# Casting and splitting two weights by one instruction, from pages kept in two hand-run regions

## The chip, the cores and the metric

The kernel runs on one core of a Trainium2 chip. The metric is the device time of one execution in microseconds (us). TensorE is PE in the profile, its weight loads PEld; VectorE is DVE, ScalarE is ACT, GpSimd is POOL, and SyncE is SP. SP and POOL issue the DMAs.

## The reference

One layer of an encoder on 256 tokens of width 2048, all in float32: a SwiGLU feed-forward block (FFN, inner width 5632), a mixer with two branches (chunked mLSTM and stick-breaking attention) merged by gates, a second FFN, and an input embedding behind a gate. A layer norm stands behind the first three.

```
x = layer_norm(ALPHA * x + 0.5 * swiglu(x, ffn1_w1, ffn1_w3, ffn1_w2))
proj = x @ w_in                        # all branches and both gates
y_m, y_sb = mlstm(...), stick_breaking(...)
merged = sigmoid(ga) * (y_m @ w_up_m) + sigmoid(gb) * (y_sb @ w_up_sb)
x = layer_norm(ALPHA * x + merged @ w_out)
x = layer_norm(ALPHA * x + 0.5 * swiglu(x, ffn2_w1, ffn2_w3, ffn2_w2))
x = x + sigmoid(x @ w_ple_gate) * (p @ w_ple_proj)
```

Weights are 528 MB of reads, each used once for 256 tokens.

## The kernel before, in words

**The arithmetic.** A float32 product is made of three matmuls of type fp32r: the activation and the weight are each split into a high part (a cast to fp32r) and a low part (the rest), and high x high, high x low, low x high are added in PSUM (L1331, L1332, L1333). A weight here is a raw page of 128 x 1024 elements (two blocks of 128 rows by 512 columns). ScalarE casts it into the high page (L1275), VectorE subtracts that from the raw page into the low page (L1279). TensorE then runs 6 matmuls on it for each of the two token halves; a product of two matrices that share the activations runs in a seven-product scheme (`seven`), in which each weight is used for one unit of 6 matmuls, and in which sums of raw pages are weights too. Such a sum is made by VectorE (L371) or by a load that adds onto a raw page that is in SBUF (`plus_load`, issued by POOL, L377). The load that adds can only be issued when the split of the page's former content is done.

**The order of the work.** The program is a list of units, written out by hand (`program`), in which side work is woven into main work (`weave`); small steps are put in by a table of delays (`DELAY`, `Sched`). Before a unit its weight is split. After each unit `splits_due` splits further weights, as long as fewer than a limit stand ready: `HELD` gives for each stage how many raw pages and how many split weights may be held at a time, for example 11 and 6 in the FFNs. Within 6 weights of a stage's end, 4 raws and 11 splits are the limit. For the first 8 weights no more than 3 are split ahead. Each engine takes its instructions in the order in which they are written.

**The pages.** All of this lies in 51 pages of 4 KB a partition, in one pool: raw pages, high and low pages, and also `big` tiles (residuals, gates, norms), `actT` tiles (activations, transposed and split). The pool hands a page out when it is free. In the mixer, ymT (the output of the mLSTM branch, four `actT` tiles) is put away in DRAM and loaded again shortly before it is used (`put_ym_away`, `bring_ym_back`, L889). That load is written just ahead of the units that read it. PSUM has 8 banks, for sums of matmuls (`mm`) and for transposes (`ms`).

Of the kernel before, what the change touches and what calls it, by code (L numbers as in the profile page):

```python
# [8 lines left out]
F32 = mybir.dt.float32  # L9
# [4 lines left out]
P = 128  # L14
# [8 lines left out]
EPS = 1e-5  # L23
COL = 512

PAGES = 51
TEMP_BUFS = 6


HELD = {"ffn": (11, 6), "mix": (6, 6), "woven": (9, 6), "wide": (11, 6)}  # L30
RAW_EDGE, SPLIT_EDGE = 4, 11
EDGE = 6

# [92 lines left out]
        return self.left.get((c, tt)) == 0  # L126


class Raw:


    def __init__(self, src, cols):
        self.src, self.cols, self.tile, self.early = src, cols, None, False


class Weight:
# [52 lines left out]
def kernel(  # L189
# [14 lines left out]
    temp_pool = ctx.enter_context(tc.tile_pool(name="temp", bufs=TEMP_BUFS))  # L204
    small = ctx.enter_context(tc.tile_pool(name="small", bufs=4))
    ps_pool = ctx.enter_context(tc.tile_pool(name="ps", bufs=PSUM_BUFS, space=bass.MemoryType.PSUM))
    ctx.enter_context(tc.manual_schedule())

    sched = Sched()
# [16 lines left out]
    def big(shape=(P, 1024)):  # L226
        return page_pool.tile(list(shape), F32, name="big", tag="page")
# [487 lines left out]
    def sb_columns(ps, t, heads):  # L715
# [3 lines left out]
        nc.scalar.copy(stage[:, :n], ps[:, :n])  # L719
        sched.spaced(sb_turn(t, stage, heads), DELAY["sbt"], BANK_GAP)  # L720

    def sv_dest(k, t):
        if ("sv", t) not in st:
            st["sv", t] = big()
        return st["sv", t][:, k * COL:(k + 1) * COL]

    def sv_ready(k, t):
# [253 lines left out]
    def stick(h):  # L981
        yield from wait(*[(n, t, h) for n in ("sq", "sk", "sv") for t in range(TT)])
        due = max(sched.now, st.get("stick", 0.0))
        st["stick"] = due + STICK_GAP
        yield bank(due - sched.now)
        q, k = st["sq", "T", h // 4][:, h % 4], st["sk", "T", h // 4][:, h % 4]
        ps = misc([P, 3 * P])
        for s in range(2):
            nc.tensor.matmul(ps[:, 256 * s:256 + P * s], k[:, s * P:(s + 1) * P], q[:, s * P:], start=True, stop=True)  # L989
        z, sp = temp(), temp()  # L990
        n = slice(0, 3 * P)
        activate(z[:, n], ps[:], ACT.Copy, scale=DS ** -0.5)
# [24 lines left out]
        ps = misc([P, S])  # L1017
        for s in range(2):
            nc.tensor.matmul(ps[:, P * s:], st["sv", s][:, h * DS:(h + 1) * DS], z[:, 256 * s:256 + P * s],  # L1019
                             start=(s == 0), stop=(s == 1))  # L1020
        parts = [(ysbT.get(h // 4, t)[:, :, h % 4], ps[:, t * P:(t + 1) * P]) for t in range(TT)]
        for dst, src in parts:
            nc.scalar.copy(dst[:, 0], src)
        for dst, src in parts:
            nc.vector.tensor_tensor(out=dst[:, 1], in0=src, in1=dst[:, 0], op=ALU.subtract)  # L1025
        for t in range(TT):
            ysbT.mark(h // 4, t, 1)
        drop()

    def in_sequence(gens):  # L1030
        for g in gens:
# [53 lines left out]

    def merge_turn(g, t):
        transposed(merged(g, t), mergedT, g, t)
        return
        yield

# [12 lines left out]
    def gate_dest(g):  # L1103
        def dest(k, t):
            if (g, t) not in gt:
                gt[g, t] = big()
            return gt[g, t][:, k * COL:(k + 1) * COL]
        return dest

# [6 lines left out]
    program.append(lambda: sched.spawn(in_sequence([gated(h) for h in range(HM)])))  # L1116
    gate = branch(0, 1)
    main = v(0) + v(1) + sb(8, 9, 2, 3) + sb(10, 11, 4, 5) + [Mode("wide")] + sb(12, 13, 6, 7) + sb(14, 15) + [lambda: sched.spawn(lane())] + branch(0, 0) + gate[:4] + bring_ym_back(gate[4:] + ups(0)) + ups(1) + ups(2)
    mode("woven")
    program.extend(weave(main, in_line([both7(w_in, sq0 + 2 * HS * DS, sq0 + 2 * HS * DS + COL, x1T, sv_dest, sv_ready, later),  # L1120
                                   both7(w_in, 3072, 3072 + COL, x1T, mo_dest, mo_ready, every), pair(1), pair(2), pair(3)])))
# [104 lines left out]
    pos = {"load": 0, "split": 0, "at": 0, "raw": 0}  # L1226

    def at_edge(j):
        return any(-EDGE <= j - e < EDGE for e in edges)
# [10 lines left out]
    def loads(most=len(raws)):  # L1240
        while pos["load"] < most and pos["raw"] < (4 if pos["at"] < 6 else limits(pos["split"])[0]):
            j = pos["load"]
            r = raws[j]
            r.tile = page_pool.tile([P, 2, COL], F32, name="raw", tag="page")
            for ks in pieces(j):
                at = 0
                for src in r.src:
                    n = src.shape[-1]
                    nc.sync.dma_start(out=r.tile[:, ks, at:at + n], in_=src[:, ks])
                    at += n  # L1250
                if j == 0 and ks.start == 0:
                    load_x(0, 1)
            pos["load"] += 1
            pos["raw"] += 1

    def make(j):
# [5 lines left out]
        if w.make and not w.made and not w.by_load and all(r.tile is not None for r in w.loads):  # L1262
            w.make()
            w.made = True

    def split_one():
# [5 lines left out]
        splits[j] = [page_pool.tile([P, 2, COL], F32R, name="split", tag="page") for _ in range(2)]  # L1272
        hi, lo = (h[:, :, :w.cols] for h in splits[j])
        for ks in pieces(j):
            nc.scalar.copy(hi[:, ks], r[:, ks])  # L1275
            make(j + 1)
            if weights[min(j + 1, len(weights) - 1)].made or not weights[min(j + 1, len(weights) - 1)].make:
                make(j + 2)
            nc.vector.tensor_tensor(out=lo[:, ks], in0=r[:, ks], in1=hi[:, ks], op=ALU.subtract)  # L1279
        pos["split"] += 1  # L1280
        for f in w.soon:
            assert f.raw.tile is not None
            f.make()
            f.made = True
        pos["raw"] -= len(w.frees)
        for r in w.frees:
            r.tile = None
# [25 lines left out]
    for u in program:  # L1313
        if isinstance(u, (Boundary, Mode)):
            continue
        if not isinstance(u, Unit):
            u()
            continue
        sched.until(lambda: u.act.ready(u.chunk, u.tt))
        j = u.tile.index  # L1320
        pos["at"] = max(pos["at"], j)
        while pos["split"] <= j:
            split_one()
        if u.start:
            u.acc["ps"] = ps_pool.tile([P, COL], F32, name="mm", tag="ps")
        ps = u.acc["ps"][:, :u.cols]
        a, w = u.act.tiles[u.chunk, u.tt], splits[j]
        for k in range(2):
            hi, lo = a[:, 0, u.sub + k], a[:, 1, u.sub + k]
            first, last = u.start and k == 0, u.stop and k == 1  # L1330
            nc.tensor.matmul(ps, hi, w[0][:, k, :u.cols], start=first, stop=False, skip_group_check=u.onto)  # L1331
            nc.tensor.matmul(ps, hi, w[1][:, k, :u.cols], start=False, stop=False, skip_group_check=u.onto)  # L1332
            nc.tensor.matmul(ps, lo, w[0][:, k, :u.cols], start=False, stop=last, skip_group_check=u.onto)  # L1333
        sched.now += 6 * 0.2161 * u.cols / COL
        u.tile.uses -= 1
        if u.tile.uses == 0:
            splits.pop(j)
        if u.stop:
            u.done(ps, u.tt)
        sched.run()  # L1340
        splits_due()
# [27 lines left out]
```

## Time and profile before

| | |
|---|---|
| median of 3 runs | 2165.42 us (2163.1 to 2165.61) |
| the profiled execution, own time | 2164.03 us |
| its span, first to last instruction | 2162.3 us, so 1.7 us lie around it |
| DVE busy | 1897.6 us (88%) |
| ACT busy | 1344.6 us (62%) |
| loads by POOL that add onto a page | 140 in the FFNs, 38 in the mixer |
| HBM | 527.85 MB read, 247 GB/s over the span |

Busy time is the sum of an engine's instructions; a group's row names the line of the kernel, the engine, the operation, what is written from what, how often, the busy time, the mean duration in ns, and the idle time of the engine just before these instructions with what ended most of it. Rows of the timeline begin with the start and the duration in us. TensorE's ends are modelled, and its matmuls overlap, so the distance from one start to the next is its pace. Loads of `w_in` are issued from 641 to 1222 us and those of `w_out` from 1240 to 1327 us, which is the mixer; the FFNs lie before and behind it, and loads of `w_ple_gate` begin at 2024 us.

### The profile page before, as it was taken

To read this page: it belongs to the slowest core of one execution; us is meant where nothing else is said; L and a number is where in the kernel's file an instruction comes from. 1 tells how busy PE (TensorE), PEld (TensorE's weight loads), DVE (VectorE), ACT (ScalarE), POOL (GpSimd) and SP (SyncE) were. 2 spreads that over 40 slices of the span, in tenths; PEclk is the share of its full clock that TensorE was granted. 3 is DMA by queue.
4 is the path that set the end of the run, shared out by engine and by line. 5 is a ranking of instruction groups with operands and counts; after the bars stand their busy time and mean duration, and the time that the engine had idled before them with its cause. 6 is when DMAs were issued, how large, how long until landed. Compare 5 with 4: busy or idle time off the path is not lost.

```text
span 2162.3 us, 27685 instructions
## 1 busy us (share of the span) xinstructions
PE 2153.1 (100%) x9798; PEld 1782.0 (82%) x9798; DVE 1897.6 (88%) x2096; ACT 1344.6 (62%) x1663; POOL 218.2 (10%) x186
## 2 busy tenths in 40 slices
PE   9999999999999999999999999999999999999999
PEld 7888888888888888888888888888888888888887
DVE  6899999999998898887888975799999999999974
ACT  7656656666665765677866563556656656666572
POOL 0111111111000000101011000011111111110000
PEclk9999999999999999999999999999999999999999
DMA  9899899999994667978898976579989999999642
GB/s 350 220 272 271 248 269 277 273 277 269 266 316 148 211 217 217 244 212 208 263 276 264 274 259 206 200 191 277 267 245 279 277 272 270 265 273 301 233 168 86
DMA packets 283179, 535.98 MB, mean 248 GB/s; under 512 B 17144, under 2 KB 34464, under 8 KB 283040
## 3 DMA queue, kind: packets, MB, share of 16 engines
q1 hardware_dynamic: 234624, 440.87, 60.0%
q0 software_dynamic: 48416, 93.33, 24.0%
q8 instruction: 77, 1.26, 0.2%
q14 instruction: 62, 0.51, 0.1%
HBM read 527.85 MB, written 6.29 MB: 247 GB/s over the span
## 4 chain that ended last, share of the span: by engine, by line
PE 91%; DVE 4%; issue 3%; DMA 2%; ACT 0%; POOL 0%; SPq 0%; DVEq 0%; POOLq 0%; ACTq 0%
PE mm L1331 29%; PE mm L1333 29%; PE mm L1332 29%; DMA raw<-in_ffn_w_dram 2%; DVE split L1279 2%; PE ms L298 1%; PE ms L524 0%; DVE actT L293 0%; POOL raw L377 0%; DVE raw L371 0%; PE ms L911 0%; PE ms L1019 0%; PE ms L989 0%; PE ms L926 0%; ACT split L1275 0%
## 5 line engine op out<-in xcount | busy, mean ns | idle before, releaser
L1275 ACT CAST split<-raw 128x1024 fp32r<-128x1024 f32 (+1 forms) x1089 | 1089.5, 1043 | 516.9 <-DMA raw<-in_ffn_w_dram 185.8
L1279 DVE TENSOR_TENSOR split<-raw,split 128x1024 fp32r<-128x1024 f32 (+1 forms) x1089 | 1277.1, 1210 | 136.6 <-ACT split L1275 128.5
L1331 PE MATMUL mm<-split,actT 128*128 128x512 f32 x3064 | 1201.2, 392 | 0.9 <-DVE actT L1025 0.9
L1333 PE MATMUL mm<-split,actT 128*128 128x512 f32 x3064 | 1187.7, 388 | 0.6 <-DVE actT L305 0.6
L1332 PE MATMUL mm<-split,actT 128*128 128x512 f32 x3064 | 1186.1, 387 | 0.4 <-DVE split L1279 0.4
L1333 PEld LDWEIGHTS mm<-split,actT 128*128 128x128 f32 x3064 | 575.1, 188 | 121.5 <-DVE actT L305 1.8
L1331 PEld LDWEIGHTS mm<-split,actT 128*128 128x128 f32 x3064 | 575.7, 188 | 115.5 <-ACT big L243 1.1
L1332 PEld LDWEIGHTS mm<-split,actT 128*128 128x128 f32 x3064 | 575.8, 188 | 114.5 <-DVE split L1279 1.7
L377 POOL DMA_DIRECT2D raw<-in_ffn_w_dram x140 | 169.7, 1440 | 1202.8 <-DVE split L1279 780.0
L371 DVE TENSOR_TENSOR raw<-raw 128x1024 f32<-128x1024 f32 x190 | 231.4, 1219 | 1.6
L377 POOL DMA_DIRECT2D raw<-in_w_in_dram x38 | 46.0, 1428 | 502.6 <-DVE split L1279 432.8
L300 ACT CAST actT<-ms 128x512 fp32r<-128x512 f32 x60 | 35.1, 586 | 73.6 <-PE ms L298 69.2
L649 DVE SCALAR_TENSOR_TENSOR big<-mm,big 128x512 f32<-128x512 f32 x112 | 76.3, 683 | 3.3 <-PE mm L1333 3.3
L597 DVE TENSOR_TENSOR temp<-mm,temp 128x512 f32<-128x512 f32 x108 | 73.1, 686 | 1.7 <-PE mm L1333 0.3
L305 DVE TENSOR_TENSOR actT<-ms,actT 128x512 fp32r<-128x512 f32 x60 | 40.9, 685 | 14.4 <-ACT big L304 9.3
L243 ACT ACTIVATE temp<-mm 128x512 f32<-128x512 f32 (+1 forms) x36 | 20.3, 569 | 49.9 <-PE mm L1333 49.9
L293 DVE TENSOR_TENSOR actT<-temp,actT 128x512 fp32r<-128x512 f32 x40 | 26.5, 687 | 17.3 <-ACT actT L292 17.2
L239 ACT ACT_TABLE_LOAD x30 | 38.5, 1283 | 0.5
L1191 DVE TENSOR_TENSOR temp<-temp,big 128x512 f32<-128x512 f32 (+1 forms) x10 | 5.8, 582 | 26.4 <-ACT temp L243 26.4
L292 ACT CAST actT<-temp 128x512 fp32r<-128x512 f32 x40 | 23.9, 620 | 8.0 <-DVE temp L316 7.4
L243 ACT ACTIVATE rstd<-mv,eps 128x1 f32<-128x1 f32 x6 | 1.8, 294 | 41.8 <-DVE mv L507 41.8
L1134 DVE SCALAR_TENSOR_TENSOR big<-big,mm 128x512 f32<-128x512 f32 x8 | 5.5, 686 | 25.3 <-PE mm L1333 25.3
(138 smaller groups left out, 613.1 us busy)
## 6 DMA issues: line engine op xcount, KB each, us to landing
raw<-in_ffn_w_dram SPq DMA_DIRECT2D x527, 512.0 KB, 7.0
raw<-in_w_in_dram SPq DMA_DIRECT2D x144, 512.0 KB, 5.1
raw<-in_ffn_w_dram POOLq DMA_DIRECT2D x140, 512.0 KB, 9.9
raw<-in_w_in_dram POOLq DMA_DIRECT2D x38, 512.0 KB, 8.4
raw<-in_w_out_dram SPq DMA_DIRECT2D x32, 512.0 KB, 5.3
raw<-in_w_ple_gate_dram SPq DMA_DIRECT2D x32, 512.0 KB, 5.0
raw<-in_w_in_dram SPq DMA_DIRECT2D x56, 256.0 KB, 4.1
raw<-in_w_up_m_dram SPq DMA_DIRECT2D x16, 512.0 KB, 6.3
```

The lines of the kernel that those rows point to most:

```text
L239: nc.scalar.preload_act_table_set(table[0])
L300: nc.scalar.copy(dst[:, 0], ps[:])
L305: nc.vector.tensor_tensor(out=dst[:, 1], in0=ps[:], in1=dst[:, 0], op=ALU.subtract)
L371: nc.vector.tensor_tensor(out=out.tile[:, :, :cols], in0=a.tile[:, :, :cols], in1=b.tile[:, :, :cols], op=ALU.add)
L377: nc.gpsimd.dma_start(out=out.tile[:, :, :cols], in_=src, accum_op=ALU.add)
L597: nc.vector.tensor_tensor(out=out, in0=a, in1=b, op=op)
L649: nc.vector.scalar_tensor_tensor(out=xs, in0=ps, scalar=0.5, in1=xs, op0=ALU.mult, op1=ALU.add)
L1275: nc.scalar.copy(hi[:, ks], r[:, ks])
L1279: nc.vector.tensor_tensor(out=lo[:, ks], in0=r[:, ks], in1=hi[:, ks], op=ALU.subtract)
L1331: nc.tensor.matmul(ps, hi, w[0][:, k, :u.cols], start=first, stop=False, skip_group_check=u.onto)
L1332: nc.tensor.matmul(ps, hi, w[1][:, k, :u.cols], start=False, stop=False, skip_group_check=u.onto)
L1333: nc.tensor.matmul(ps, lo, w[0][:, k, :u.cols], start=False, stop=last, skip_group_check=u.onto)
```

## The change

Of the 51 pages, 10 raw pages and 12 split pages are taken out of the pool and become two tiles of their own, `raws` and `splits`, which a free list (`Region`) hands out by number; the pool keeps 29. Two weights that follow each other, both of full width and both in pages of `raws`, are cast by one ScalarE instruction over both pages (L1371) and subtracted by one VectorE instruction (L1373); an access pattern with the distance of the two pages as its step makes that possible. Such a pair is split when two weights' room is free. A weight that doesn't qualify is split alone (L1349, L1351), as before. Two page-sized tiles of the mixer (the attention's `sv` and one gate tile) lie in `raws` for a while. The number of raws in one stretch of the mixer ("wide") goes from 11 to 9.

```diff
+RAWS = 10
+SPLITS = 12
+PAGES = 51 - RAWS - SPLITS
-HELD = {"ffn": (11, 6), "mix": (6, 6), "woven": (9, 6), "wide": (11, 6)}
+HELD = {"ffn": (11, 6), "mix": (6, 6), "woven": (9, 6), "wide": (9, 6)}
+class Region:
+    def take(self, n, like=None):
+        at = [self.free.pop(0) for _ in range(n)]
+        if like:
+            at.sort(reverse=like[0] > like[1])
+        return at
+    def give(self, pages):
+        self.free += [p for p in pages if p is not None]
+    def both(self, at):
+        a, b = sorted(at)
+        return self.tile[:, a:b + 1:b - a]
...
+    def lent(name):
+        st["page", name], = raw_pages.take(1)
+        pos["keep"] = int(name != (2, 0))
+        return raw_pages.tile[:, st["page", name]]
...
-            r.tile = page_pool.tile([P, 2, COL], F32, name="raw", tag="page")
+            if len(raw_pages.free) > pos["keep"]:
+                r.page, = raw_pages.take(1)
+                r.tile = raw_pages.sheet(r.page)
+            else:
+                r.tile = page_pool.tile([P, 2, COL], F32, name="raw", tag="page")
...
+    def two(j):
+        if j == 0 or j + 1 >= len(weights) or at_edge(j) or at_edge(j + 1):
+            return False
+        a, b = weights[j:j + 2]
+        if min(a.cols, b.cols) < COL or None in (a.raw.page, b.raw.page) or a.raw is b.raw:
+            return False
+        ahead(j)
+        return whole(j) and whole(j + 1)
+
+    def split_two():
+        j = pos["split"]
+        at = [w.raw.page for w in weights[j:j + 2]]
+        his, los = split_pages.take(2, at), split_pages.take(2, at)
+        r, hi, lo = raw_pages.both(at), split_pages.both(his), split_pages.both(los)
+        nc.scalar.copy(hi, r)
+        ahead(j + 2)
+        nc.vector.tensor_tensor(out=lo, in0=r, in1=hi, op=ALU.subtract)
...
+        for k in range(2):
+            through(j + k)
+        loads()
 
     def splits_due():
         most = pos["at"] + 3 if pos["at"] < 8 else len(weights)
-        while pos["split"] < most and len(splits) < limits(pos["split"])[1]:
-            split_one()
+        while pos["split"] < most:
+            room = limits(pos["split"])[1] - len(splits)
+            if pos["split"] + 1 < most and two(pos["split"]):
+                if room < 2 or len(split_pages.free) < 4:
+                    break
+                split_two()
+            elif room < 1:
+                break
+            else:
+                split_one()
```

Of the 1071 splits of full pages, 906 go into 453 pairs and 165 stay alone (counted in the built program, on ScalarE and on VectorE alike). TensorE's instructions are the same, in the same order. Three places show what moves on the engines around it; numbers tell tiles apart, and in brackets stand the engines and queues that an instruction waits for.

VectorE at the start of the kernel, before: `L305` are the low parts of the activations, `L1279` the low parts of weights 0 (in two halves), 1, 2, 3.

```order
L305 TENSOR_TENSOR actT_120<-ms_115,actT_120 128x512 [waits PE_49,Activation_49]
L1279 TENSOR_TENSOR split_126<-raw_99,split_125 128x512 [waits DMAHW1_49,Activation_49]
L1279 TENSOR_TENSOR split_126<-raw_99,split_125 128x512 [waits DMAHW3_49,Activation_49]
L305 TENSOR_TENSOR actT_138<-ms_133,actT_138 128x512 [waits PE_49,Activation_49]
L1279 TENSOR_TENSOR split_143<-raw_103,split_142 128x1024 [waits DMAHW4_49,Activation_49]
L1279 TENSOR_TENSOR split_149<-raw_107,split_148 128x1024 [waits DMAHW7_49,Activation_49]
L305 TENSOR_TENSOR actT_177<-ms_172,actT_177 128x512 [waits PE_49,Activation_49]
```

The same place now:

```order
L332 TENSOR_TENSOR actT_118<-ms_113,actT_118 128x512 [waits PE_49,Activation_49]
L1351 TENSOR_TENSOR splits_73<-raws_72,splits_73 128x512 [waits DMAHW1_49,Activation_49]
L1351 TENSOR_TENSOR splits_73<-raws_72,splits_73 128x512 [waits DMAHW3_49,Activation_49]
L332 TENSOR_TENSOR actT_133<-ms_128,actT_133 128x512 [waits PE_49,Activation_49]
L1373 TENSOR_TENSOR splits_73<-raws_72,splits_73 128x2048 [waits DMAHW7_49,DMAHW4_49,Activation_49]
L332 TENSOR_TENSOR actT_164<-ms_159,actT_164 128x512 [waits PE_49,Activation_49]
```

Weights 1 and 2 are one instruction, and it waits for both loads, that on queue DMAHW4 and that on DMAHW7.

SP in the mixer, at the last of the four loads that bring ymT back, before:

```order
L1249 DMA raw_10027<-in_w_up_sb_dram 128x2x512 [waits DMAHW0_49,DVE_49,PE_49]
L1249 DMA raw_10039<-in_w_in_dram 128x2x512 [waits DMAHW1_49,DMASW3_49,DVE_49]
L1249 DMA raw_10072<-in_w_up_sb_dram 128x2x512 [waits DMAHW2_49,PE_49]
L889 DMA actT_10074<-ymaway_91 128x1024 [waits DMAHW3_49,PE_49]
L1249 DMA raw_10093<-in_w_in_dram 128x2x512 [waits DMAHW4_49,PE_49]
```

The same place now, on SP:

```order
L1296 DMA raw_8017<-in_w_in_dram 128x2x512 [waits PE_49]
L1296 DMA raws_72<-in_w_up_sb_dram 128x2x512 [waits DMAHW0_49,DMASW3_49]
L924 DMA actT_8045<-ymaway_93 128x1024 [waits DMAHW7_49,DVE_49]
L1296 DMA raws_72<-in_w_in_dram 128x2x512 [waits DMAHW2_49]
L1296 DMA raws_72<-in_w_up_sb_dram 128x2x512 [waits DMAHW3_49]
```

and on VectorE, the instructions up to the one for which this load waits:

```order
L398 TENSOR_TENSOR raws_72<-raws_72,raw_8017 128x1024 [waits DMAHW7_49]
L1373 TENSOR_TENSOR splits_73<-raws_72,splits_73 128x2x1024 [waits DMAHW6_49,Activation_49]
L452 TENSOR_TENSOR big_7957<-mm_7771,big_7957 128x512 [waits DVE_49]
L458 TENSOR_SCALAR big_7957<-big_7957,mm_7746 128x512 [waits DVE_49]
L452 TENSOR_TENSOR raws_72<-mm_7820,raws_72 128x512 [waits PE_49]
L1373 TENSOR_TENSOR splits_73<-raws_72,splits_73 128x2048 [waits DMAHW0_49,Activation_49]
L1351 TENSOR_TENSOR splits_73<-raw_8017,splits_73 128x1024 [waits Activation_49]
```

The load waited for a matmul before; now it waits for VectorE's split of `raw_8017`, whose pool page it gets.

TensorE in the mixer, where a PSUM bank is handed on, before:

```order
L1332 MATMUL mm_7879<-split_8085,actT_6990 128x512
L1333 MATMUL mm_7879<-split_8084,actT_6990 128x512
L733 MATMUL ms_8179<-ident_76,temp_8129 128x128 [waits Activation_49]
L733 MATMUL ms_8179<-ident_76,temp_8129 128x128 x3
L1331 MATMUL mm_8193<-split_8065,actT_6044 128x512 [waits DVE_49]
```

and now:

```order
L1432 MATMUL mm_6242<-splits_73,actT_5536 128x512
L1433 MATMUL mm_6242<-splits_73,actT_5536 128x512
L768 MATMUL ms_6491<-ident_78,temp_6444 128x128 [waits Activation_49]
L768 MATMUL ms_6491<-ident_78,temp_6444 128x128 x3
L1431 MATMUL mm_6499<-splits_73,actT_4735 128x512 [waits PE_49,Activation_49]
```

The sum `mm_6499` now gets the bank of the transposes `ms_6491` that stand right ahead of it, and waits for ScalarE to copy them out; before it got another bank, freed by VectorE.

More of the change, by code (lines that the diff above doesn't have):

```diff
@@ L1028, in stick @@
         drop()
+        st["sticks"] = st.get("sticks", 0) + 1
+        if st["sticks"] == HS:
+            back(("sv", 0))
     def in_sequence(gens):
@@ L1225 @@
     splits = {}
-    pos = {"load": 0, "split": 0, "at": 0, "raw": 0}
+    pos = {"keep": 0, "load": 0, "split": 0, "at": 0, "raw": 0}
     def at_edge(j):
@@ L1264, in make, with through, whole, ahead @@
             w.made = True
+    held = {}
+    def through(j):
+        w = weights[j]
+        for f in w.soon:
+            assert f.raw.tile is not None
+            f.make()
+            f.made = True
+        pos["raw"] -= len(w.frees)
+        for r in w.frees:
+            raw_pages.give([r.page])
+            r.tile = r.page = None
+    def whole(j):
+        w = weights[min(j, len(weights) - 1)]
+        return w.made or not w.make
+    def ahead(j):
+        make(j)
+        if whole(j):
+            make(j + 1)
     def split_one():
@@ L1271, in split_one @@
         r = w.raw.tile[:, :, :w.cols]
-        splits[j] = [page_pool.tile([P, 2, COL], F32R, name="split", tag="page") for _ in range(2)]
+        if len(split_pages.free) > 1:
+            held[j] = split_pages.take(2)
+            splits[j] = [split_pages.sheet(n) for n in held[j]]
+        else:
+            splits[j] = [page_pool.tile([P, 2, COL], F32R, name="split", tag="page") for _ in range(2)]
         hi, lo = (h[:, :, :w.cols] for h in splits[j])
@@ L1275, in split_one @@
             nc.scalar.copy(hi[:, ks], r[:, ks])
-            make(j + 1)
-            if weights[min(j + 1, len(weights) - 1)].made or not weights[min(j + 1, len(weights) - 1)].make:
-                make(j + 2)
+            ahead(j + 1)
             nc.vector.tensor_tensor(out=lo[:, ks], in0=r[:, ks], in1=hi[:, ks], op=ALU.subtract)
         pos["split"] += 1
[L1281 to L1287, printed above, removed]
+        through(j)
+        loads()
[16 more added lines that the diff above has]
+        for k in range(2):
+            held[j + k] = [his[k], los[k]]
+            splits[j + k] = [split_pages.sheet(n) for n in held[j + k]]
+        pos["split"] += 2
+        for k in range(2):
+            through(j + k)
         loads()
```

22 lines of the change are left out of this document (18 added, 4 removed).

## The prediction

> **What bounds the kernel now.** I read the page first: busy time by engine and the chain that ended last.
>
> ```profile
> span 2162.3 us, 27685 instructions
> PE 2153.1 (100%) x9798; PEld 1782.0 (82%) x9798; DVE 1897.6 (88%) x2096; ACT 1344.6 (62%) x1663; POOL 218.2 (10%) x186
> ...
> PE 91%; DVE 4%; issue 3%; DMA 2%; ACT 0%; POOL 0%; SPq 0%; DVEq 0%; POOLq 0%; ACTq 0%
> ```
>
> TensorE is in work for 2153.1 of 2162.3 us, and 91% of the chain is its. A modelled end could hide gaps, so I read its waits next (line, who was waited for, us in total, times, longest).
>
> ```profile
> PE ms L1209 <- DVE ones L247: 1.1, 1, 1.1
> PE mm L1331 <- DVE actT L1025: 0.9, 1, 0.9
> PE ms L298 <- DMA big<-in_x_dram: 0.7, 1, 0.7
> PE mm L1333 <- DVE actT L305: 0.6, 2, 0.3
> PE mm L1332 <- DVE split L1279: 0.4, 1, 0.4
> PE ms L298 <- DVE actT L305: 0.4, 1, 0.4
> ```
>
> These are all, 4.1 us together, 1.8 of them before the first product; only 0.4 us is a wait for a split. Last, TensorE's pace, from its timeline in the mixer and in a stretch where VectorE has little to do.
>
> ```profile
> 1150.58 0.39 PE L1331 MATMUL mm<-split,actT 128*128 128x512 f32 x1
> 1151.26 0.39 PE L1331 MATMUL mm<-split,actT 128*128 128x512 f32 x1
> ...
> 1320.24 0.39 PE L1331 MATMUL mm<-split,actT 128*128 128x512 f32 x1
> 1320.92 0.39 PE L1331 MATMUL mm<-split,actT 128*128 128x512 f32 x1
> ...
> 1296.00:1350.00 54.00, 54.00 (x239) 44.45 (x238) 29.75 (x32) 22.78 (x23) 0.00 (x0) 1.00 0.63 205
> ```
>
> From L1331 to the next L1331 are three matmuls in 0.68 us both times, 0.227 us each, although in the second stretch VectorE is busy for only 29.75 of 54 us, ScalarE for 22.78. TensorE runs at its own pace, which the splitting doesn't touch; time saved on ScalarE and VectorE can only win from the 4.1 us. A measurement of this kernel tells about 0.2%, 4.3 us. What can move the time is whether a split still comes in time.
>
> **The pairs.** Their durations come from two instructions that stand back to back.
>
> ```profile
> 245.13 2.36 DVE L1279 TENSOR_TENSOR split<-raw,split 128x1024 fp32r<-128x1024 f32 x2
> ...
> 1152.59 2.01 ACT L1275 CAST split<-raw 128x1024 fp32r<-128x1024 f32 x2 [3.32 <-PE mm L1332]
> ...
> L1275 ACT CAST split<-raw 128x1024 fp32r<-128x1024 f32 (+1 forms) x1089 | 1089.5, 1043 | 516.9 <-DMA raw<-in_ffn_w_dram 185.8 <-DVE raw L371 155.3 <-PE mm L1332 76.5
> L1279 DVE TENSOR_TENSOR split<-raw,split 128x1024 fp32r<-128x1024 f32 (+1 forms) x1089 | 1277.1, 1210 | 136.6 <-ACT split L1275 128.5 <-PE mm L1332 2.9 <-DMA raw<-in_w_in_dram 2.3
> ```
>
> A pair costs at most 2.36 us on VectorE and 2.01 us on ScalarE; I take 2.28 and 1.95. The saving, 0.06 to 0.14 us by 453 pairs, some 30 to 60 us on each engine, is work beside TensorE's and counts nothing. [...] What a pair does cost is lateness: its first weight is ready only when both raws have landed and both are cast and subtracted, 0.9 + 1.07 us later than alone.
>
> **The start: +4.8 us.** Weights 1 and 2 become a pair.
>
> ```profile
> 8.57 1.05 ACT L1275 CAST split<-raw 128x1024 fp32r<-128x1024 f32 x1
> 11.74 1.05 ACT L1275 CAST split<-raw 128x1024 fp32r<-128x1024 f32 x1 [2.12 <-DMA raw<-in_ffn_w_dram]
> ...
> 9.66 1.22 DVE L1279 TENSOR_TENSOR split<-raw,split 128x1024 fp32r<-128x1024 f32 x1 [0.35 <-ACT split L1275]
> ...
> 10.90 0.48 PE L1331 MATMUL mm<-split,actT 128*128 128x512 f32 x1
> 11.22 0.39 PE L1332 MATMUL mm<-split,actT 128*128 128x512 f32 x1
> ```
>
> Weight 1 was cast at 8.57 and used at 10.90 (high part) and 11.22 us (low part). The raw of weight 2 lands at 11.74: ScalarE waited for it. The loads stand in the same order, so the pair is cast from 11.74 to 13.7 and subtracted to 16.0 us: L1332 starts 16.05 - 11.22 = 4.8 us later. No gap stands behind it that could take this back, since the later waits for L305 (0.6 us) hang on transposes that TensorE itself makes. Bounds 3.8 (that 0.6 and small restarts absorbed) and 5.
>
> **The last ymT load: +10 us.** It now waits for VectorE's split of `raw_8017`, whose cast waits for the last matmul on `mm_8128`, the one ahead of the first reader of the loaded tile. So TensorE stops while a cast, a split and a load run one after the other.
>
> ```profile
> 1141.48 0.42 SPq L889 DMA_DIRECT2D actT<-ymaway  x1
> ...
> DMA to landing us min/median/max: 4.7/5.8/6.9
> ...
> raw<-in_w_in_dram SPq DMA_DIRECT2D x144, 512.0 KB, 5.1
> ...
> 1150.63 0.68 DVE L425 TENSOR_TENSOR big<-mm,big 128x512 f32<-128x512 f32 x1
> ...
> L371 DVE TENSOR_TENSOR raw<-raw 128x1024 f32<-128x1024 f32 x190 | 231.4, 1219 | 1.6
> ```
>
> Before, it was issued at 1141.48 and its tile first read at 1151.26 (the L1331 quoted above): 9.8 us for 5.8, no wait. Now, from the end of the matmul: cast 1.05, split 1.21, load 5.8 and an estimated 0.2 for four hand-overs (cast to split took 257.76 - 256.67 - 1.05 = 0.04 in the rows further down), 8.3 us, with the fastest load 7.1. VectorE comes later than that: `raw_8017` is issued 42 matmuls, 9.5 us, ahead and lands 5.1 later, 4.4 us before the stop; then VectorE still has a sum (L371's kind, 1.22), a pair (2.28), three of L425's kind (3 x 0.65) and a pair (2.28), 7.7 us, so that it reaches the split 3.3 us behind the stop, 2.2 behind the cast. With that 8.3 becomes 10.5; some of it will overlap, I take 10, bounds 7 and 12. The stop gives what is queued behind on SP more time than it loses. [...]
>
> **The PSUM hand-over: +1 us.** `mm_6499` waits for two copies of the kind L738, of 0.37 us each, and for two hand-overs.
>
> ```profile
> L738 ACT COPY big<-ms x16: 344/372/380, 737.6 to 1061.4; 128x256 f32<-128x256 f32 x16
> ```
>
> That is 0.74 + 0.3, 1 us, more if a pair is on ScalarE (bound 2). A second hand-over of this kind stands where TensorE already waited 0.9 us for L1025: nothing.
>
> **The loads that add: +9 us.** In the FFNs a chain runs split, load that adds, cast, split, matmul.
>
> ```profile
> 246.71 2.44 POOL L377 DMA_DIRECT2D raw<-in_ffn_w_dram  x2 [32.01 <-DVE split L1279]
> ...
> 256.67 1.05 ACT L1275 CAST split<-raw 128x1024 fp32r<-128x1024 f32 x1 [2.88 <-DMA raw<-in_ffn_w_dram]
> ...
> 257.76 1.23 DVE L1279 TENSOR_TENSOR split<-raw,split 128x1024 fp32r<-128x1024 f32 x1 [2.32 <-ACT split L1275]
> ...
> 262.28 0.39 PE L1332 MATMUL mm<-split,actT 128*128 128x512 f32 x1
> ```
>
> From the issue at 246.71 to the cast are 10.0 us, the low part is ready at 258.99, TensorE reads it at 262.28: 3.3 us to spare, in one of the tightest. With pairs the chain grows by 1.07 + 0.9 + 1.07 = 3.0 us, and counted in matmuls of the unchanged order, from the one that frees a page to the one that needs the load, it has 17 us where it had 18.3 (the shortest in each). 3.3 - 3.0 - 1.3 = -1.0 us: the tightest are late by about 1 us. There are 9 blocks of seven products in each FFN; a stop in one lets its other chains catch up, so I count half of 18 at 1 us each: 9. Bounds 0 (the shorter queue on VectorE gives it back) and 18 blocks x 2 = 36.
>
> **The sum.** 4.8 + 10 + 1 + 9 = 25 us onto the profiled execution's own 2164.0 (span and 1.7 around it): 2189, and as the median of the runs lies 1.4 us above that execution, 2190.
>
> **Rivals.** *A, the loads that add decide* (chance 0.18): if landing goes late with the fuller bursts of two raws, all 18 blocks lose 1.5 to 2.5 us: 27 to 45 in place of 9, 2208 to 2226. For it, in the page's slices, the busy share of the DMA engines in tenths:
>
> ```profile
> DMA  9899899999994667978898976579989999999642
> ```
>
> In most of the FFNs' slices it is 0.9 or more. Against: the same bytes in the same time.
> *B, only the mixer and start count* (0.16): the chains hold as before, and the ymT load comes at its lower bound: 3.8 + 7 + 1, 2177.
> *C, not slower: TensorE's pace* (0.06): 0.227 us a matmul might hold waits for SBUF, behind ScalarE and VectorE. With 42% fewer split instructions it would have to fall by 2.7 ns to 0.2243 to win 25 us over the 9192 products and end at 2165; beyond that, faster. Against it: the pace was the same at 29.75 us of VectorE in 54. [...]
> The rest (0.60) is the forecast, 2190, its own range 2180 to 2207.
>
> **The numbers.** Range 2174 to 2212: it takes in B, the forecast and the lower part of A. Slower by over 0.2% holds for the forecast, A and B, 0.94, less something for a step read wrongly: 0.90; within 0.2%: 0.05; faster: 0.05.
>
> **What would show it.** In the changed profile: L1332 of weight 1 near 16 us; a wait of TensorE for the DMA from `ymaway` of 7 to 12 us, the longest of all; a wait of about 1 us for L773; waits for L1371 and L1373 in the FFNs of some 9 us in all; VectorE's busy time down by 30 to 70 us; matmuls still 0.227 us apart. I am wrong if TensorE's waits stay near 4 us, or if a single one above 3 us stands elsewhere.

## The result, and the profile after

The changed kernel takes 2321.8 us (median, 2320.4 to 2322.8), the one before in the same session 2165.5: ratio 1.072, 95% interval 1.070 to 1.074. It is slower by 156 us; the forecast was 2190 with a range of 2174 to 2212. Times in this text are medians of executions that agree within 0.5%; a single one that took 7770 us, of a later version (a pair's subtract as two instructions), is left out.

The page of the changed kernel, its span, its busy time by engine, and the chain that ended last:

```profile
span 2318.7 us, 26169 instructions
PE 2238.2 (97%) x9798; PEld 1785.9 (77%) x9798; DVE 1873.0 (81%) x1643; ACT 1300.2 (56%) x1210; POOL 217.2 (9%) x186
...
PE 54%; issue 17%; DVE 13%; DMA 11%; ACT 4%; POOL 1%; SPq 0%; ACTq 0%; POOLq 0%; DVEq 0%
```

VectorE and ScalarE have 25 and 44 us less to do, as the change meant. TensorE does the same 9798 matmuls and is busy for 85 us longer, and its share of the chain that ended last is 54% where it was 91%. Its waits (line, who was waited for, us in total, times, longest):

```profile
PE mm L1432 <- DVE splits L1373: 56.0, 52, 2.2
PE mm L1431 <- DMA actT<-ymaway: 8.1, 1, 8.1
PE mm L1431 <- ACT splits L1371: 3.1, 3, 2.2
...
PE mm L1431 <- ACT big L773: 0.7, 1, 0.7
```

L1371 and L1373 are the cast and the subtract of a pair, L773 the copy of transposes out of PSUM. TensorE waited for a split 0.4 us before, and now 56 us in 52 places. But all its waits come to some 75 us of 156, so I looked at the distance between matmuls that wait for nothing, in the timeline of the mixer:

```profile
1160.03 0.39 PE L1431 MATMUL mm<-splits,actT 128*128 128x512 f32 x1
...
1166.33 0.39 PE L1431 MATMUL mm<-splits,actT 128*128 128x512 f32 x1
```

Nine rounds of three matmuls lie between the two rows: 6.30 us / 27 = 0.2333 us each, and 0.227 before. This holds throughout: of all distances of 0.220 to 0.245 us between the starts of 512-column products, the mean is 227.2 ns over 8,695 before and 233.2 over 8,495 after. That is some 6.0 ns x 8,500 = 51 us.

One place in an FFN shows the stops (start, duration, engine; in brackets the idle time ahead and what ended it):

```profile
641.12 1.91 ACT L1371 CAST splits<-raws 128x2048 fp32r<-128x2048 f32 x1 [7.33 <-DMA raws<-in_ffn_w_dram]
643.06 2.29 DVE L1373 TENSOR_TENSOR splits<-raws,splits 128x2048 fp32r<-128x2048 f32 x1 [4.91 <-ACT splits L1371]
645.40 0.50 PE L1432 MATMUL mm<-splits,actT 128*128 128x512 f32 x1 [1.82 <-DVE splits L1373]
...
656.55 1.23 DVE L398 TENSOR_TENSOR raws<-raws,raw 128x1024 f32<-128x1024 f32 x1
657.94 1.91 ACT L1371 CAST splits<-raws 128x2048 fp32r<-128x2048 f32 x1 [5.22 <-DVE raws L398]
659.89 2.29 DVE L1373 TENSOR_TENSOR splits<-raws,splits 128x2048 fp32r<-128x2048 f32 x1 [0.91 <-ACT splits L1371]
662.23 0.50 PE L1432 MATMUL mm<-splits,actT 128*128 128x512 f32 x1 [1.03 <-DVE splits L1373]
```

The high page exists when the cast ends (643.03) and TensorE starts on it; the low page of the same weight exists only 2.29 us later, when the subtract of both is over. The second time the chain is sum, cast, subtract, on two engines that take turns. Over the kernel the turns read so in the waits of these engines:

```profile
ACT splits L1371 <- DVE raws L398: 290.8, 103, 6.6
DVE splits L1373 <- ACT splits L1371: 267.0, 170, 7.0
```

Before, the same two waits were 155.3 and 128.5 us (in the group rows of the cast and the subtract that the prediction shows). Counted in distances between matmul starts, the 156 us are: 51 us for the slower pace, 83 us more in 75 distances of over 0.47 us (88 less 5 before), 10 us in some 50 matmuls that run at half speed, 0.43 us apart, behind a long stop, and some 12 in small ones.

### The profile page after: what moved, and what is told of

Read it like the earlier page. It is cut to its first block, busy times and chain, and to the rows that moved or that the text cites. A ratio compares the mean times of both kernels' runs of the same rounds, so it can differ in the third digit from the quotient of the medians.

```text
span 2318.7 us, 26169 instructions
## 1 busy us (share of the span) xinstructions
PE 2238.2 (97%) x9798; PEld 1785.9 (77%) x9798; DVE 1873.0 (81%) x1643; ACT 1300.2 (56%) x1210; POOL 217.2 (9%) x186
## 4 chain that ended last, share of the span: by engine, by line
PE 54%; issue 17%; DVE 13%; DMA 11%; ACT 4%; POOL 1%; SPq 0%; ACTq 0%; POOLq 0%; DVEq 0%
PE mm L1432 17%; PE mm L1433 17%; PE mm L1431 17%; DMA raws<-in_ffn_w_dram 10%; DVE splits L1373 8%; ACT splits L1371 3%; DVE raws L398 2%; POOL raws L404 1%; DVE splits L1351 1%; DVE temp L624 1%; PE ms L325 1%; ACT temp L270 1%; DVE big L676 0%; DMA raws<-in_w_in_dram 0%; PE ms L551 0%
## 5 line engine op out<-in xcount | busy, mean ns | idle before, releaser
L1373 DVE TENSOR_TENSOR splits<-raws,splits 128x2048 fp32r<-128x2048 f32 x453 | 1032.0, 2288 | 310.5 <-ACT splits L1371 267.0
L1432 PE MATMUL mm<-splits,actT 128*128 128x512 f32 (+1 forms) x2992 | 1187.5, 397 | 57.0 <-DVE splits L1373 56.0
L1371 ACT CAST splits<-raws 128x2048 fp32r<-128x2048 f32 x453 | 858.7, 1910 | 626.2 <-DVE raws L398 290.8
L1431 PE MATMUL mm<-splits,actT 128*128 128x512 f32 (+1 forms) x2992 | 1193.7, 399 | 13.9 <-DMA actT<-ymaway 8.1
L1433 PE MATMUL mm<-splits,actT 128*128 128x512 f32 (+1 forms) x2992 | 1179.5, 394 | 0.5 <-DVE actT L332 0.5
L1432 PEld LDWEIGHTS mm<-splits,actT 128*128 128x128 f32 x2992 | 565.1, 189 | 212.1 <-DVE splits L1373 85.9
L1431 PEld LDWEIGHTS mm<-splits,actT 128*128 128x128 f32 x2992 | 565.1, 189 | 147.2 <-DMA actT<-ymaway 8.5
L1433 PEld LDWEIGHTS mm<-splits,actT 128*128 128x128 f32 x2992 | 565.2, 189 | 132.0 <-DVE actT L332 1.4
L404 POOL DMA_DIRECT2D raws<-in_ffn_w_dram x128 | 158.5, 1446 | 1213.4 <-DVE splits L1373 1036.3
L398 DVE TENSOR_TENSOR raws<-raws 128x1024 f32<-128x1024 f32 x157 | 191.3, 1220 | 4.0 <-DMA raws<-in_w_in_dram 2.2
L1349 ACT CAST splits<-raws 128x1024 fp32r<-128x1024 f32 (+2 forms) x84 | 80.7, 967 | 55.7 <-PE mm L1433 40.9
L1349 ACT CAST splits<-raw 128x1024 fp32r<-128x1024 f32 (+1 forms) x81 | 84.5, 1043 | 41.5 <-PE mm L1433 19.8
L1351 DVE TENSOR_TENSOR splits<-raws,splits 128x1024 fp32r<-128x1024 f32 (+2 forms) x84 | 92.8, 1114 | 12.5 <-ACT splits L1349 12.3
L1351 DVE TENSOR_TENSOR splits<-raw,splits 128x1024 fp32r<-128x1024 f32 (+1 forms) x81 | 98.2, 1213 | 4.2 <-ACT splits L1349 3.7
```

What stands on the lines that cost most here:

```text
L398: nc.vector.tensor_tensor(out=out.tile[:, :, :cols], in0=a.tile[:, :, :cols], in1=b.tile[:, :, :cols], op=ALU.add)
L404: nc.gpsimd.dma_start(out=out.tile[:, :, :cols], in_=src, accum_op=ALU.add)
L1371: nc.scalar.copy(hi, r)
L1373: nc.vector.tensor_tensor(out=lo, in0=r, in1=hi, op=ALU.subtract)
```

## The experiments

The first four ask whether the pace comes from where the pages stand in SBUF, and whether the stops come from the pairs or from the fixed regions.

**The regions moved by 64 bytes.** All pages stood at byte 192 of a 256-byte line before (a line here is no more than the byte address counted modulo 256). The two region tiles, allocated ahead of the other constants, stand at byte 128, while the stationary operands (`actT`, in the shared pool) stay at 192.

```diff
-    raw_pages = Region(consts.tile([P, RAWS, 2 * COL], F32, name="raws"))
-    split_pages = Region(consts.tile([P, SPLITS, 2 * COL], F32R, name="splits"))
...
     nc.gpsimd.affine_select(bound[:], bound[:], ...)
+    raw_pages = Region(consts.tile([P, RAWS, 2 * COL], F32, name="raws"))
+    split_pages = Region(consts.tile([P, SPLITS, 2 * COL], F32R, name="splits"))
```

> The changed kernel with one thing different: the tiles of the 10 raw and 12 split pages are allocated behind the other constants, so that each page starts 64 bytes further on, at byte 192 of a 256-byte line (as all pages did before) instead of byte 128. The instructions, their order and their waits stay. Theory 'address' (the 512-column matmul takes 233 ns instead of 227 because its moving operand stands at another offset): the matmuls fall back to about 226.7 ns, 0.0066 us x some 8,700 = 57 us go, about 2,265 us. Rival 'company' (the matmuls are slower because ScalarE and VectorE now read and write 2,048-column tiles beside them): 233 ns and about 2,322 us stay. In both the waits of TensorE for the pairs' subtract (56 + 86 us in the two rows) stay within a fifth.

2305.0 us, ratio 1.065 (1.063 to 1.066). Its timeline in an FFN and its longest wait:

```profile
635.67 0.39 PE L1431 MATMUL mm<-splits,actT 128*128 128x512 f32 x1
...
637.03 0.39 PE L1431 MATMUL mm<-splits,actT 128*128 128x512 f32 x1
...
PE mm L1432 <- DVE splits L1373: 80.9, 76, 2.4
```

The pace is back: 1.36 us for six matmuls, 0.227 each, with the same long instructions beside it, so the company of ScalarE and VectorE isn't its cause. The time hardly followed: 17 us of the 57 expected. The part of the expectation that failed is that the waits stay: a faster TensorE reaches the late pages sooner and waits 80.9 us instead of 56.0. Counted in distances of over 0.47 us between matmul starts, less the usual 0.23 each, the stops grow from 88 to 121 us.

**No pairs, pages where the change puts them.**

```diff
-            if pos["split"] + 1 < most and two(pos["split"]):
+            if False and two(pos["split"]):
```

> The changed kernel with its regions of pages kept, but every weight cast and split by itself, as before. Theory 'pairs make TensorE wait' (two engines alternate over the pair, and a pair needs the room of two weights before it begins): the waits of L1432 for the subtract go down from 56 us (and 86 us on the weight-load side) to under 10, some 80 us less: about 2,240 us. Rival 'the fixed division into pages makes TensorE wait' (10 raw and 12 split pages that can't be lent to each other): the waits stay within a fifth, and the time stays near 2,320 us. In both the matmuls stay near 233 ns, since the pages stand where they stood.

2225.2 us, ratio 1.028 (1.026 to 1.030), 97 us less than the change. These are the two longest of TensorE's waits:

```profile
PE mm L1431 <- DMA actT<-ymaway: 5.9, 1, 5.9
PE ms L1252 <- DVE ones L274: 1.1, 1, 1.1
```

No wait for a split is left, and the matmuls are 233 ns apart as expected: the stops belong to the pairs, the pace doesn't.

**The kernel before with all pages at byte 128.**

```diff
+    small = ctx.enter_context(tc.tile_pool(name="small", bufs=4))
     page_pool = ctx.enter_context(tc.tile_pool(name="page", bufs=PAGES))
...
-    small = ctx.enter_context(tc.tile_pool(name="small", bufs=4))
...
+    both = consts.tile([P, 2 + P], F32, name="both")
+    eps, bound = both[:, 1 + P:2 + P], both[:, 0:1 + P]
...
```

> The kernel before with the same instructions, but all its pages start at byte 128 of a 256-byte line instead of 192 (the small pool stands ahead of the pages, and eps in a spare column of bound). The stationary operands move with them. Theory 'address of the moving operand': matmuls 233 ns instead of 227, some 55 us more, about 2,220 us. Rival 'the two operands of a matmul must stand at the same offset': 227 ns and 2,165 us stay. Rival 'company': 227 ns and 2,165 us stay.

2165.1 us, ratio 1.000 (0.999 to 1.001), and its matmuls are 227.2 ns apart. My theory of the moving operand's own address falls: at byte 128 it is as fast as at 192 (227.2 ns both times), where the stationary operand stands there too.

**Matmuls alone, by the two offsets.** 72 in a row for each pair of offsets, in the layer's order of operands, nothing else running; m is the byte of the moving page in its 256-byte line, s that of the stationary one.

> Not the layer: 72 matmuls each, three per pair of moving and stationary pages as in the layer and with nothing beside them, with the moving page at 0, 32, 64 ... 224 bytes past a 256-byte line (stationary at 192), then the stationary page at 0, 64, 128, 192 with the moving one at 128 and at 192. Theory 'address of the moving operand': 233 ns at 128 and 227 ns at 192 whatever the stationary's place, and some offset may be faster than 227. Rival 'relation of the two': the time depends on the difference, so moving 128 with stationary 128 gives 227 ns. Rival 'company': all alike at 227 ns or below.

The timeline, at the first matmul of each stretch that is used here; a stretch ends where the next begins:

```profile
87.60 0.40 PE L40 MATMUL m128s192x<-mov,sta 128*128 128x512 f32 x1
...
104.41 0.40 PE L40 MATMUL m160s192x<-mov,sta 128*128 128x512 f32 x1
...
121.20 0.39 PE L40 MATMUL m192s192x<-mov,sta 128*128 128x512 f32 x1
...
137.54 0.40 PE L40 MATMUL m224s192x<-mov,sta 128*128 128x512 f32 x1
...
237.43 0.39 PE L40 MATMUL m128s64x<-mov,sta 128*128 128x512 f32 x1
...
253.92 0.39 PE L40 MATMUL m128s128x<-mov,sta 128*128 128x512 f32 x1
...
270.25 0.40 PE L40 MATMUL m128s192x<-mov,sta 128*128 128x512 f32 x1
```

Moving at 128 with stationary at 192, as in the changed kernel: 16.81 us / 72 = 233.5 ns. At 192 with 192: 16.34 / 72 = 226.9; at 128 with 128: 226.8; at 128 with 64: 229.0. In all stretches the time goes with the distance of the two, modulo 256: 227 ns at 0, 229 where the moving page is 64 bytes on, 232 to 234 at the other multiples of 32. The rival "relation of the two" holds. That the profile's clock is full in the stretches compared (1.00) says that it isn't the clock; what in the memory makes it so isn't shown.

The next five take the pairs apart, all with the regions moved so that the pace is right.

**No pairs and the regions moved.** Both edits above together.

> The changed kernel with its regions of pages, but both suspects taken out: every weight cast and split by itself, and the regions behind the other constants so that moving and stationary pages stand at the same byte of a 256-byte line. Theory 'offset and pairs make up the whole loss': matmuls 227 ns (57 us less than with the pairs out alone), no waits of L1432: 2,165 to 2,172 us. Rival 'the regions cost something too' (10 raw and 12 split pages that are not lent to each other): over 2,180 us. The same could show a second way: as in the run with the regions moved and the pairs kept, a faster TensorE may only wait more, which would leave more than 20 us of the 57.

2187.1 us, ratio 1.010 (1.009 to 1.012). The pairs cost 2305.0 - 2187.1 = 118 us here, the pace 2225.2 - 2187.1 = 38. The rival holds as well: some 22 us stay, most of them in three waits that come to 16.7 us here and to 0.8 in the kernel before:

```profile
PE ms L325 <- DVE actT L332: 6.5, 6, 2.0
PE mm L1431 <- DMA actT<-ymaway: 6.2, 1, 6.2
PE mm L1432 <- DVE splits L1351: 4.0, 6, 1.1
```

**Pairs only where no sum is due.**

```diff
-        ahead(j)
-        return whole(j) and whole(j + 1)
+        return not weights[j].make and not weights[j + 1].make
```

> The changed kernel with the regions behind the constants, and pairs made only of weights of which neither has a sum to be made on VectorE first: 215 pairs instead of 453. Theory 'lock-step' (a pair's cast waits for two sums that wait for the pair's subtract before, so the two engines take turns): the waits of L1432 for a pair's subtract, 81 us with all pairs, fall below 20 us, the time to about 2,200 us. Rival 'length' (the pair's own cast and subtract, 1.9 and 2.3 us, are late whatever stands ahead of them): the waits fall with the number of pairs, to about 38 us, the time to about 2,230 us.

2209.2 us, ratio 1.020 (1.019 to 1.022), and the wait that was 80.9 us:

```profile
PE mm L1431 <- DVE splits L1372: 17.3, 16, 2.6
```

215 pairs cost 22 us, 0.10 us each; the 238 others cost 96, 0.40 each. This is what lock-step expected of the waits (below 20 us, not 38); the time stays 9 us above its 2,200. If the two add up, a pair beside sums is four times as dear. The edit also leaves single the weights whose sum a load makes, so this run doesn't tell the sums of VectorE from the loads that add.

**A pair's subtract as two instructions, and a pair's cast as two.**

```diff
-        nc.vector.tensor_tensor(out=lo, in0=r, in1=hi, op=ALU.subtract)
+        for k in range(2):
+            nc.vector.tensor_tensor(out=split_pages.sheet(los[k]), in0=raw_pages.sheet(at[k]),
+                                    in1=split_pages.sheet(his[k]), op=ALU.subtract)
```

> The changed kernel with the regions behind the constants; the pair is cast by one instruction, but subtracted by two, a weight each, at the same place of the program. The first weight's low page is then ready some 1.1 us sooner (2.29 less 1.2), the second's not later by more than 0.1. Theory 'the pair's subtract is what L1432 waits for': of some 75 stalls of 1.1 us each most go, and the raw of the first comes free sooner: 2,302 falls by 60 to 90 us, to about 2,225. Rival 'the pair's cast is the length that counts': the stalls stay within a third, about 2,285 us.

2283.8 us, ratio 1.054 (1.052 to 1.057): 21 us less, where I expected 60 to 90.

```diff
-        nc.scalar.copy(hi, r)
+        for k in range(2):
+            nc.scalar.copy(split_pages.sheet(his[k]), raw_pages.sheet(at[k]))
```

> The changed kernel with the regions behind the constants; two casts, a weight each, and then one subtract for the pair. Theory 'the pair's subtract is what L1432 waits for': little changes, the first weight's low page comes no sooner, about 2,290 us (the casts cost ScalarE some 0.15 us more a pair, the first of them may start before the second weight's sum). Rival 'the pair's cast is the length that counts' (it can't begin until both raws are whole): about 2,230 us.

2266.7 us, ratio 1.047 (1.046 to 1.049): 38 us less, between the two theories. Shortening either link alone gives 21 and 38 of 118 us, and neither "the subtract" nor "the cast" is the cause by itself.

**Both as two, at the pair's place in the program.** Cast, subtract, cast, subtract; both sums still stand ahead, and room for two weights is still asked for.

```diff
-        nc.scalar.copy(hi, r)
-        ahead(j + 2)
-        nc.vector.tensor_tensor(out=lo, in0=r, in1=hi, op=ALU.subtract)
+        for k in range(2):
+            nc.scalar.copy(split_pages.sheet(his[k]), raw_pages.sheet(at[k]))
+            if k:
+                ahead(j + 2)
+            nc.vector.tensor_tensor(out=split_pages.sheet(los[k]), in0=raw_pages.sheet(at[k]),
+                                    in1=split_pages.sheet(his[k]), op=ALU.subtract)
```

> The changed kernel with the regions behind the constants; a pair keeps its place in the program (both sums made first, room for two weights, both raws there), but is cast and split by two and two instructions: cast, subtract, cast, subtract. Theory 'the long instructions' (nothing of a pair can be used before the cast and the subtract of both are over): with all of it a weight at a time the waits go as with no pairs at all, 2,187 us and at most 2,200. Rival 'the order' (both sums ahead of the first cast, and two weights' room and raws): the time stays near that of the kernel with the pairs cast singly, 2,266 us, and at least 2,245.

2209.7 us, ratio 1.021 (1.020 to 1.023), short of both expectations and nearer to the first.

```profile
PE mm L1435 <- DVE splits L1375: 12.5, 15, 2.5
PE mm L1434 <- DMA actT<-ymaway: 8.3, 1, 8.3
```

Taken out in this order, the joined instructions make 95 of the 118 us (2305.0 - 2209.7) and the order with its room 23 (2209.7 - 2187.1). The 95 are more than 21 + 38: with both short, a cast can run beside the subtract of the weight ahead of it. In the traces, casts and subtracts of weights run at the same time for 573 us with two instructions a pair, 601 with the subtract as two, 632 with the cast as two, 704 with both as two, and 706 without pairs. VectorE's wait for the cast shrinks with it (first row: four instructions a pair; second row: two):

```profile
DVE splits L1375 <- ACT splits L1372: 163.5, 121, 3.8
```
```profile
DVE splits L1373 <- ACT splits L1371: 275.0, 161, 7.4
```

**No pairs and small regions.** The regions are moved as above, with 4 raw and 8 split pages instead of 10 and 12; 39 pages are shared.

```diff
-RAWS = 10
-SPLITS = 12
+RAWS = 4
+SPLITS = 8
```

> No pairs, the regions behind the constants, but of 4 raw and 8 split pages instead of 10 and 12, so that 39 pages are shared in place of 29. Theory 'the fixed division' (the 22 us left without pairs are waits for pages that stand free in the other region): the wait for the ymT load (6.2 us) and those for L332 (6.5 us) go back towards the kernel before, which has none and 0.4: 2,165 to 2,177 us. Rival 'the limits in the table of held raws and the two lent pages': 2,183 us or more stay.

2171.3 us, ratio 1.003 (1.002 to 1.004): 16 of the 22 us go, and no wait for `ymaway` is left: the fixed division made most of what stayed. What makes the last 6 us isn't shown. Its longest waits are now

```profile
PE ms L1054 <- DVE temp L906: 1.6, 1, 1.6
PE mm L1432 <- DVE split L1351: 1.3, 1, 1.3
```

**The first pair left single**, in the kernel with pairs only where no sum is due.

```diff
-        if j == 0 or j + 1 >= len(weights) or at_edge(j) or at_edge(j + 1):
+        if j <= 1 or j + 1 >= len(weights) or at_edge(j) or at_edge(j + 1):
```

> The kernel with pairs only where no sum is due, and without the pair of weights 1 and 2. Theory 'the start costs what weight 2's load is late': L1432 of weight 1 starts near 11.3 us and not near 16, and 4 to 5 us go, 2,209 to about 2,204.5 us. Rival 'taken back later' (the later start lets the loads behind it run ahead): less than 2 us go.

2202.3 us, ratio 1.018 (1.017 to 1.020), 7 us less, as expected within what the runs tell apart (2206.2 to 2211.3 against 2201.9 to 2207.8). The start's stop is gone.

**Matmuls alone, smaller distances.**

> Not the layer: 72 matmuls each as in the earlier measurement, with the moving page at byte 192 of a 256-byte line and the stationary page 0, 4, 8, 16, 24, 48, 240, 248 and 252 bytes further on; then both pages at byte 0, 64, 4 and 32. Theory 'the distance of the two, modulo 256, sets the pace': 227 ns at distance 0 and wherever both stand alike; small distances between 227 and 234 ns, none faster than 226. Rival 'only whole 64-byte parts count': distances of 4 to 24 bytes cost as little as 0. If some distance were under 220 ns, the layer could be made faster than before by shifting its pages.

Stretches of 72 again (d4: stationary 4 bytes further on than moving; "sameac": both at byte 4), each beginning and what follows it:

```profile
21.61 0.39 PE L40 MATMUL d0x<-mov,sta 128*128 128x512 f32 x1
...
37.95 0.39 PE L40 MATMUL d4x<-mov,sta 128*128 128x512 f32 x1
...
54.68 0.40 PE L40 MATMUL d8x<-mov,sta 128*128 128x512 f32 x1
...
121.45 0.39 PE L40 MATMUL d240x<-mov,sta 128*128 128x512 f32 x1
...
137.90 0.39 PE L40 MATMUL d248x<-mov,sta 128*128 128x512 f32 x1
...
203.72 0.39 PE L40 MATMUL sameacx<-mov,sta 128*128 128x512 f32 x1
...
220.82 0.39 PE L40 MATMUL sameadx<-mov,sta 128*128 128x512 f32 x1
```

Distance 0 gives 226.9 ns, 4 bytes 232.4; with the stationary page 16 bytes behind the moving one (d240), it is 228.5. The rival in which only whole 64-byte parts count falls with the 232.4. Both at byte 4 give 237.5 although they stand alike, so the first theory is wrong there: the distance alone sets the pace only where both stand at multiples of 32 bytes, as far as these runs go. No stretch whose time is given here was faster than 226.8 ns, so no shift of pages shown here beats the kernel before, and none of the versions here does.

## Why the prediction was wrong

- **The start** (+4.8 us) held as a stop. ScalarE casts the pair when raw 2 has landed, and L1432 comes at 16.10 us where it came at 11.22:

```profile
11.82 1.90 ACT L1371 CAST splits<-raws 128x2048 fp32r<-128x2048 f32 x1 [3.22 <-DMA raws<-in_ffn_w_dram]
13.75 2.29 DVE L1373 TENSOR_TENSOR splits<-raws,splits 128x2048 fp32r<-128x2048 f32 x1 [4.42 <-ACT splits L1371]
16.10 0.80 PE L1432 MATMUL mm<-splits,actT 128*128 128x512 f32 x1 [1.82 <-DVE splits L1373]
```

  The sum had nothing for what follows: the granted clock is 0.50 from 16 to 20 us and 0.71 from 20 to 24, by which I estimate another 4 x 0.50 + 4 x 0.29 = 3 us.

- **The last ymT load** (+10, bounds 7 and 12) held with 8.1 us, by the mechanism given: VectorE's split ends, SP issues the load in the next 0.02 us, TensorE waits for it. VectorE reaches that split 3.5 us behind the stop (3.3 in the prediction), but TensorE goes on 3.3 us after the load's issue, for which the sum had 5.8; so its wait was set too long by the load. With the 2 us at half clock behind the stop (last section) the cost comes to 10 all the same, which is luck.

```profile
1234.50 1.22 DVE L1351 TENSOR_TENSOR splits<-raw,splits 128x1024 fp32r<-128x1024 f32 x1
1235.74 0.34 SPq L924 DMA_DIRECT2D actT<-ymaway  x1
1239.07 0.79 PE L1431 MATMUL mm<-splits,actT 128*128 128x512 f32 x1 [8.06 <-DMA actT<-ymaway]
```

  It belongs to the fixed regions: it is 6.2 us without pairs and gone with small regions.
- **The PSUM hand-over** (+1) held with the 0.7 us for L773 shown above.
- **"TensorE runs at its own pace, which the splitting doesn't touch"** is the first step that failed. The evidence for it, the same 0.227 us in a stretch with a less busy VectorE (29.75 of 54 us), spoke against contention and against nothing else; the change also moved the pages from byte 192 to 128, away from the stationary operand. This is worth 51 us of the 156 in the changed kernel's own distances, 38 with the pairs out, 17 with them in. Rival C doubted the same step, but looked for a gain, from waits behind ScalarE and VectorE that no run shows: with the regions moved, the 0.227 us came back with the same instructions beside it.
- **"The loads that add: +9 us"** is the second. I priced one chain, through the loads that add, in half of 18 blocks. What stopped TensorE was every pair that came just in time, whatever its load: its low page follows the high one by 2.29 us where it was 1.2, and cast and subtract wait for each other. Followed back one by one in the changed kernel's trace, 9 of the 52 waits for a pair's subtract (10.6 of 56.0 us) stand behind a cast that had waited for a load that adds, 24 (23.3 us) behind a cast that had waited for a sum of VectorE, and 19 (22.1 us) behind neither. So the chain that was priced came near its 9 us in TensorE's waits, and the chains left out made the loss. The sentence that the saving "is work beside TensorE's and counts nothing" was right of the saving, but the joined instructions also take away the overlap of the two engines (573 us of it where 706 were without pairs). The pairs cost 118 us (95 of them the joining) once the pace is right, against 9 and the start's 4.8 forecast, and 36 as the upper bound of the 9; rival A, 27 to 45 us, kept to the loads that add as well.
- **A pair's own cost** held: mean 2.288 and 1.910 us in these group rows, where I took 2.28 and 1.95.

```profile
L1371 ACT CAST splits<-raws 128x2048 fp32r<-128x2048 f32 x453 | 858.7, 1910 | 626.2 <-DVE raws L398 290.8 <-PE mm L1433 147.2 <-DMA raws<-in_ffn_w_dram 134.0
L1373 DVE TENSOR_TENSOR splits<-raws,splits 128x2048 fp32r<-128x2048 f32 x453 | 1032.0, 2288 | 310.5 <-ACT splits L1371 267.0 <-PE mm L1433 29.4 <-DMA raws<-in_w_out_dram 7.3
```

  VectorE's busy time fell by 25 us, though, less than the 30 to 70 that I expected. The saving worked out from the trace was 30 to 60; no run shows the 70.

## What to carry to other kernels

Two instructions that are joined over two pages are also two pages that become ready late and together: price that against the engine that reads them, and for every page that comes just in time, not only for the tightest chain. A change of an allocation is a change of addresses: where tiles leave their pool, compare the bytes at which both operands of a matmul stand (here matmuls with both at multiples of 32 took 226.9 ns where the distance was a multiple of 256 bytes, 229 to 234 where it wasn't), and see in the trace whether the pace between matmuls is still the same. When one of two losses is mended and the time hardly moves, look whether the other has grown into the room.

## What was not expected of the hardware

In the matmuls alone, of 512 columns with a weight load each and with both operands at multiples of 32 bytes, the pace went with the distance of the two in SBUF: 226.9 ns at a multiple of 256 bytes, 229 to 234 at other multiples of 32.

A stop also cost time behind itself. Behind the ymT stop the granted clock is a half (windows: length, PE, PEld, VectorE, ScalarE and GpSimd busy, clock, DMA share, GB/s):

```profile
1234.00:1239.00 5.00, 0.00 (x0) 0.00 (x0) 1.72 (x2) 0.00 (x0) 0.00 (x0) 0.50 0.43 152
1239.00:1243.00 4.00, 3.94 (x9) 3.13 (x10) 0.00 (x0) 0.00 (x0) 0.00 (x0) 0.50 0.89 272
```

and ten matmuls are 0.43 us apart, 10 x 0.2 = 2 us.

Shorter stops did it too, by where they lay. The stretches at half clock in this trace begin whole multiples of 3.413 us apart. I cut the trace into steps of that length and added up TensorE's idle time in each. From 20 us to the last matmul, and where the clock had been full, a step with 1.82 us of idle or more was followed by half clock every time (five steps), and none with 1.79 us or less was. The stop that ends at 645.40 us above lay wholly in one step and was followed by 3.41 us at half clock; the one that ends at 576.94 us, of 1.83 us, had 1.70 of them in one step and was not. So in this trace 1.82 us of idle within one step of 3.413 us, about half of it, was enough.
